# Output projection of a two-layer diffusion step: norms half a block apart, heads rounded straight out of PSUM, first inner block of the FFN in three token pieces

## The chip, the cores and the metric

The kernel runs on one core of a Trainium2 chip. The metric is the device time of one execution in microseconds (us), taken as the median of three runs. Five engines work side by side and meet at semaphores: PE (matrix multiplication, with its weight loads shown apart as PEld), DVE (vector), ACT (scalar functions and copies), POOL (a second, slower vector engine) and SP, whose queue issues the DMA transfers.

## The reference

One step of a two-layer model over 1152 tokens: 1024 latent tokens and a prompt of 128, width 1024. Layer 0 (in the names below l = 0) has differential attention, layer 1 sliding-window attention. What the change touches is what follows attention in each layer:

```python
o = rmsnorm(o, subln_g) * (1.0 - lam_init)         # layer 0 alone, one norm per head of 128
y = o @ w_o                                        # output projection, 1024 x 1024
x = x + gate1 * rmsnorm(y, g1)                     # post_norm_residual
h = rmsnorm(x, g2) * (1 + scale) + shift           # pre_norm_modulate
y = (silu(h @ w_gate) * (h @ w_up)) @ w_down       # SwiGLU, inner width 2816
x = x + gate2 * rmsnorm(y, g3)
```

## The kernel before

Tokens are worked on in nine blocks of 128, in the order `OORDER` = 0, 1, 4, 5, 2, 6, 3, 7, 8 (8 is the prompt). A program fixes the order on PE, ACT, DVE and POOL: what is written first in the code is issued first on its engine. Only the DMA queue is ordered by a scheduler.

Every fp32 operand of a large product is split in a rounded part ("h" in its name) and the rest ("l"), and a product is three matmuls: h by h, h by l, l by h.

**Output projection.** `OProj.step(i)` runs once for each of the nine places i, from -2 on, and lists its parts with an offset k, so that a step works on several blocks at once. `turn` of block i+1: eight PE transposes of the attention result V into the PSUM tile tp_o (L1312; tag "t", two banks), an ACT copy into the SBUF tile o32 (L1314 in layer 0, L1316 in layer 1), a rounding by POOL into oh (L110) and a DVE subtraction into ol (L1318). `norms(0)` of block i-1: sum of squares of the projected block by ACT (L127). `stat` of block i+2, in layer 0 alone: eight ACT squares, one per head (L1265). `proj` of block i: 48 matmuls in two halves (L1326 to L1328) into the PSUM tiles oacc. Between the halves `scale` (layer 0: square root, then POOL multiplies V by the head norms, L1281) and the norms of block i-1: `norms(1)` is a root (L135), a reciprocal (L137), DVE's scaling of oacc by two instructions (L153), POOL's or DVE's addition to the residual (L154) and the sum of squares of the result K by ACT (L127); `norms(2)` ends it on DVE (L145, L146) and gives xn. "Hooks" are pieces of other work hung on the halves of a step: the prompt's attention, the first pairs of tokens for the FFN (in steps 5 and 6), and the preparation of FFN weights.

**FFN, up.** 22 inner blocks d of 128 gate and 128 up columns. Instead of eight quarter products, each is worked out by seven (a Strassen form): names B11, B21, T2, T3, T1, B22, T4, into the PSUM tiles guX (tag "b", four banks), guY ("t", two) and guZ ("u", two). The tokens, folded in half, form two parts of 256 and 320 columns (`PARTS`). Weights are prepared by `prep`: for the Strassen sums POOL adds quarters (L1470 to L1477), ACT rounds (L1488) and DVE subtracts (fl, L1490), and the small "u" (L1480, L1481). For the tokens, `Halves.pair` takes two blocks: PE transposes xn into tp_n (L1388, two tiles, tag "u"), `first` rounds them by ACT (L1395) and copies them raw by DVE (L1396), `second` makes the sums and all rounded parts and rests (L1406 to L1421).

Part 0 (blocks 0, 4, 1, 5) is made in steps 5 and 6. Part 1 (blocks 2 with 6, 3 with 7, and the prompt) is made by the list `late` between the products of d = 0, part 0. Then d = 0 runs part 1, and from d = 1 on both parts follow each other product by product. `sums` takes the products out of PSUM (ACT L1534 to L1550, DVE L1536 to L1554).

Of the kernel before, what the change touches and what calls it, by code (L numbers as in the profile page):

```python
# [44 lines left out]
def hybrid_step(ctx: ExitStack, tc: tile.TileContext, x_prompt, x_sample, cache_diff_k, cache_diff_v,  # L45
# [1193 lines left out]
    class OProj:  # L1239
# [63 lines left out]
        def turn(self, tb):  # L1303
            i = OORDER.index(tb) % 2 * 2
            oh, ol = self.ohl[tb] = [self.room(f"w{i + f}", [P, KB, P], F32R, "oh") for f in range(2)]
            o32 = self.room("r1", [P, KB, P], F32, "o32")
            for half in range(2):
                ks = slice(half * 4, half * 4 + 4)
                tp = self.ps.tile([P, 4, P], F32, name="tp_o", tag="t", bufs=2)
                for j in range(4):  # L1310
                    kb = half * 4 + j
                    pe.transpose(tp[:, j, :], self.o[tb][:, kb * P:(kb + 1) * P], ident)  # L1312
                if self.l == 0:
                    act.activation(out=o32[:, ks, :], in_=tp, func=AF.Copy, scale=subg)  # L1314
                else:
                    act.copy(out=o32[:, ks, :], in_=tp)  # L1316
                pool_round(oh[:, ks, :], o32[:, ks, :])
                dve.tensor_tensor(out=ol[:, ks, :], in0=o32[:, ks, :], in1=oh[:, ks, :].bitcast(F32), op=ALU.subtract)  # L1318

# [10 lines left out]
        def norms(self, tb, part):  # L1330
            gg, G, sh = self.mod(tb)
            if part == 0:
                self.xn[tb] = self.room(f"x{OORDER.index(tb) % 5}", [P, D], F32, "xn")
                self.ss[tb] = sumsq(self.acc[tb], junk)
            elif part == 1:
                rs, x = rstd(self.ss[tb]), self.xt[tb]
                post_norm(self.acc[tb], rs, gg, x, x, self.xn[tb], dve if OORDER.index(tb) < 2 else pool)
                dma(out=x_d[tb * P:(tb + 1) * P, :], in_=x)
                self.ss[tb] = sumsq([x], junk)
            else:  # L1340
                pre_norm(rstd(self.ss[tb]), self.xt[tb], G, sh, self.xn[tb], dve)
# [21 lines left out]
    PARTS = (256, 320)  # L1363

    A_COLS = {(0, 0): ((0, 256, 0),), (0, 1): ((0, 256, 256),), (1, 0): ((0, 320, 512),),
              (1, 1): ((0, 256, 896), (256, 320, 832))}

    class Halves:
# [23 lines left out]
        def first(self, part, c, a, raw):  # L1392

            for i, name in enumerate(("B11", "B21")):
                act.copy(out=self.hi[name, part][:, :, c:c + a[i].shape[-1]], in_=a[i])  # L1395
                dve.tensor_copy(out=raw[:, i], in_=a[i])  # L1396

        def second(self, part, c, b, raws):
# [23 lines left out]
            high("T4", T)  # L1422
            for name, x in (("B11", B11), ("B21", B21), ("T1", T1), ("T2", T2), ("B22", B22), ("T4", T)):
                low(name, x)
# [18 lines left out]
    class Ffn:  # L1443
# [18 lines left out]
        def prep(self, d, what):  # L1462
# [15 lines left out]
            elif what == "u":  # L1478
                u = w[d, "u"] = rooms.take((P, D), F32R, "fhl")
                act.copy(out=u[:, 0:512], in_=A22)  # L1480
                dve.tensor_tensor(out=u[:, 512:D], in0=A22, in1=u[:, 0:512].bitcast(F32), op=ALU.subtract)  # L1481
                rooms.give(w[d, "r", 1])
# [16 lines left out]
        def product(self, d, k, part):  # L1499
            to, i, half, name = self.PRODUCTS[k]  # L1500
            n = PARTS[part]
            acc = self.acc

# [7 lines left out]
            if i == 1:  # L1511
                hi, lo = [self.w[d, "u"][:, f * 512:(f + 1) * 512] for f in range(2)]
# [3 lines left out]
            xh, xl = self.hv.hi[name, part], self.hv.lo[name, part]  # L1516
            for kb in range(4):
# [6 lines left out]
        def post(self, name, part):  # L1524
            t = self.pt.tile([P, 320], F32, name=name, tag=name, bufs={"s1": 3, "sg": 3 - self.l}.get(name, 2))
            return t[:, 0:PARTS[part]]

        def sums(self, d, k, part):

            acc, t, n = self.acc, self.sums_of.setdefault(part, {}), PARTS[part]  # L1530
            X, Y, Z = [acc[to, part][:, 0:n] if (to, part) in acc else None for to in "XYZ"]
# [30 lines left out]
        def free(self, d, k):  # L1562
            if k in self.DONE:
                self.rooms.give(*[self.w[d, f, self.DONE[k]] for f in "hl"])
            elif k == 6:
                self.rooms.give(self.w[d, "u"])

# [3 lines left out]
        def up(self, tasks, mroom, late, pt, ahead):  # L1571
# [161 lines left out]
    class Layer:  # L1733
# [8 lines left out]
        def begin(self, stack):  # L1742
# [15 lines left out]
            def pair(part, c, *tbs):  # L1758
                rooms = [where[f"x{OORDER.index(tb) % 5}"] for tb in tbs]
                yield from f.hv.pair(part, c, [op.xn[tb] for tb in tbs], [*rooms, *self.temps][:3])  # L1760
                if part:
                    f.rooms.free += rooms
                yield
# [11 lines left out]
            with tc.manual_schedule(engines=ENGINES):  # L1775
# [18 lines left out]
                f.rooms.free.insert(0, self.temps[0])  # L1794
# [9 lines left out]
        def ffn(self, tasks):  # L1804

            l, f, op, H = self.l, self.f, self.op, self.H
            with ExitStack() as high:
# [3 lines left out]
                for tag in names:  # L1811
# [4 lines left out]
                R.tile([P, 512], F32, name="room", tag="mw", bufs=2)  # L1816
                self.temps = [macc, (R, "mw", 2)]
# [183 lines left out]
```

## Time and profile before

| | |
|---|---|
| median of three runs | 3203.99 us (3201.15 to 3204.88) |
| the profiled execution's own time | 3199.07 us |
| its span in the trace | 3197.3 us |
| mean granted PE clock | 0.981 |
| PE busy | 3001.8 us, 94% of the span |
| DVE, ACT, POOL busy | 64%, 44%, 43% |
| longest chain | PE 67%, POOL 14%, DVE 9%, ACT 4% |

Times inside an execution are read in the trace as microseconds from the start of the span. The output projection of layer 0 with the first inner block behind it lies from about 834 to 1022.6 us, that of layer 1 from about 2264 to 2442.2 us. In 40 slices of the span the digit of PE falls to 8 in and behind these two places (and in the attention of layer 0).

### The profile page before, as it was taken

To read this page: it belongs to the slowest core of one execution; us is meant where nothing else is said; L and a number is where in the kernel's file an instruction comes from. 1 tells how busy PE (TensorE), PEld (TensorE's weight loads), DVE (VectorE), ACT (ScalarE), POOL (GpSimd) and SP (SyncE) were. 2 spreads that over 40 slices of the span, in tenths; PEclk is the share of its full clock that TensorE was granted. 3 is DMA by queue.
4 is the path that set the end of the run, shared out by engine and by line. 5 is a ranking of instruction groups with operands and counts; after the bars stand their busy time and mean duration, and the time that the engine had idled before them with its cause. 6 is when DMAs were issued, how large, how long until landed. Compare 5 with 4: busy or idle time off the path is not lost.

```text
span 3197.3 us, 47914 instructions
## 1 busy us (share of the span) xinstructions
PE 3001.8 (94%) x17998; PEld 2636.8 (82%) x17998; DVE 2048.6 (64%) x2789; ACT 1421.9 (44%) x2764; POOL 1361.9 (43%) x1186
## 2 busy tenths in 40 slices
PE   8999988998896999999999899999987999999999
PEld 5888777777776999999878787777767999998887
DVE  6786388888566777753786643999567633334544
ACT  6332267777554333333444323777433333333442
POOL 2553289999343444442021343666333433340101
PEclk9999999999998999999999999999988999999999
DMA  6675633332422434335765354433432322226564
GB/s 214 200 228 179 201 112 114 116 118 94 130 100 80 129 109 129 109 97 177 252 216 195 130 173 125 116 115 99 142 107 81 108 64 83 66 80 211 185 199 149
DMA packets 373808, 442.23 MB, mean 138 GB/s; under 512 B 26804, under 2 KB 295644, under 8 KB 373576
## 3 DMA queue, kind: packets, MB, share of 16 engines
q1 hardware_dynamic: 373576, 439.16, 43.6%
q8 instruction: 142, 2.33, 0.3%
q14 instruction: 90, 0.74, 0.1%
HBM read 335.71 MB, written 103.37 MB: 137 GB/s over the span
## 4 chain that ended last, share of the span: by engine, by line
PE 67%; POOL 14%; DVE 9%; ACT 4%; issue 3%; DMA 2%; SPq 1%; DVEq 0%; ACTq 0%; POOLq 0%
POOL aT L784 7%; PE guX L1518 6%; PE guX L1519 6%; PE guX L1520 6%; PE dacc L1635 5%; PE dacc L1637 5%; PE dacc L1636 5%; POOL aT L110 4%; PE qacc L556 4%; PE qacc L558 4%; PE qacc L557 4%; PE guY L1518 3%; PE guY L1520 3%; PE guY L1519 3%; PE guZ L1518 1%
## 5 line engine op out<-in xcount | busy, mean ns | idle before, releaser
L1551 POOL TENSOR_TENSOR sg<-sg,U 128x256 f32<-128x256 f32 x88 | 74.9, 851 | 563.4 <-ACT sg L1550 553.1
L1635 PE MATMUL dacc<-fh,ahl 128*128 128x512 f32 x792 | 312.0, 394 | 2.3 <-DVE U L1554 2.3
L1636 PE MATMUL dacc<-fl,ahl 128*128 128x512 f32 x792 | 310.7, 392 | 0.0
L1637 PE MATMUL dacc<-fh,ahl 128*128 128x512 f32 x792 | 310.7, 392 | 0.0
L556 PE MATMUL qacc<-whi,hh 128*128 128x512 f32 x648 | 259.7, 401 | 1.3 <-ACT hh L431 1.3
L558 PE MATMUL qacc<-whi,hl 128*128 128x512 f32 x648 | 254.9, 393 | 0.0
L557 PE MATMUL qacc<-wlo,hh 128*128 128x512 f32 x648 | 254.2, 392 | 0.6 <-DVE wlo L106 0.6
L154 POOL TENSOR_TENSOR xt<-yacc,xt 128x1024 f32<-128x1024 f32 (+1 forms) x19 | 49.7, 2621 | 459.9 <-DVE yacc L153 242.0
L784 POOL TENSOR_TENSOR aT<-a,aT 128x512 fp32r<-128x512 f32 x186 | 237.3, 1276 | 15.5
L1620 DVE TENSOR_TENSOR fl<-fraw,fh 128x1024 fp32r<-128x1024 f32 x132 | 165.4, 1253 | 121.3 <-ACT fh L1619 120.7
L744 DVE TENSOR_REDUCE nm<-S 128x1 f32<-128x1280 f32 x128 | 190.2, 1486 | 51.1 <-PE S L737 51.1
L1619 ACT CAST fh<-fraw 128x1024 fp32r<-128x1024 f32 x132 | 138.4, 1048 | 170.8 <-DMA fraw<-in_w_down_dram 156.7
L737 PE MATMUL S<-K,q 128*128 128x512 f32 (+1 forms) x768 | 184.5, 377 | 12.9 <-ACT e L749 8.9
L266 DVE SCALAR_TENSOR_TENSOR macc<-wmod,sc,macc 128x512 f32<-128x512 f32 x196 | 186.1, 992 | 0.0
L1635 PEld LDWEIGHTS dacc<-fh,ahl 128*128 128x128 f32 x792 | 149.2, 188 | 36.4 <-DVE U L1554 3.1
L1637 PEld LDWEIGHTS dacc<-fh,ahl 128*128 128x128 f32 x792 | 149.0, 188 | 33.7
L1636 PEld LDWEIGHTS dacc<-fl,ahl 128*128 128x128 f32 x792 | 149.1, 188 | 32.9
L749 ACT ACTIVATE e<-S,nm 128x1280 f32<-128x1280 f32 x128 | 171.4, 1339 | 7.2 <-DVE nm L744 7.1
L737 PEld LDWEIGHTS S<-K,q 128*128 128x128 f32 x768 | 137.5, 193 | 43.8 <-ACT e L749 19.0
L578 ACT CAST xT<-tpx 128x512 fp32r<-128x512 f32 x127 | 68.5, 592 | 236.5 <-issue 125.3
L110 POOL TENSOR_SCALAR aT<-a 128x512 fp32r<-128x512 f32 x192 | 154.0, 802 | 22.7 <-ACT a L773 22.7
L1490 DVE TENSOR_TENSOR fl<-fsum,fh 128x1024 fp32r<-128x1024 f32 x84 | 102.3, 1218 | 81.3 <-ACT fh L1488 81.3
(369 smaller groups left out, 9726.7 us busy)
## 6 DMA issues: line engine op xcount, KB each, us to landing
fraw<-in_w_down_dram SPq DMA_DIRECT2D x132, 512.0 KB
wmod<-in_w_mod_dram SPq DMA_DIRECT2D x112, 256.0 KB
araw<-a_d SPq DMA_DIRECT2D x132, 192.0 KB
fraw<-in_w_gate_dram SPq DMA_DIRECT2D x44, 512.0 KB
fraw<-in_w_up_dram SPq DMA_DIRECT2D x42, 512.0 KB
qT_d<-xT SPq DMA_DIRECT2D x36, 512.0 KB
q<-qT_d SPq DMA_DIRECT2D x64, 256.0 KB
wraw<-in_w_qkv_diff_dram SPq DMA_DIRECT2D x24, 512.0 KB
```

What stands on the lines that cost most here:

```text
L110: pool.tensor_scalar(out=out, in0=in_, scalar1=1.0, scalar2=0.0, op0=ALU.mult, op1=ALU.add)
L556: pe.matmul(acc, lhsT=xh, rhs=hi[:, a, :], start=(kb == 0), stop=False)
L557: pe.matmul(acc, lhsT=xh, rhs=lo[:, a, :], start=False, stop=False)
L558: pe.matmul(acc, lhsT=xl, rhs=hi[:, a, :], start=False, stop=(kb == KB - 1))
L737: pe.matmul(S[:, j:j + n], lhsT=self.q[:, f, m, i * P:(i + 1) * P], rhs=kv[self.h][0][:, m, j:j + n], start=(f == 0), stop=(f == 1))
L784: (dve if self.last else pool).tensor_tensor(out=lo, in0=x, in1=hi.bitcast(F32), op=ALU.subtract)
L1518: pe.matmul(o, lhsT=hi[:, kb, :], rhs=xh[:, kb, :], start=(first and kb == 0), stop=False, **more)
L1519: pe.matmul(o, lhsT=hi[:, kb, :], rhs=xl[:, kb, :], start=False, stop=False, **more)
L1520: pe.matmul(o, lhsT=lo[:, kb, :], rhs=xh[:, kb, :], start=False, stop=(kb == 3), **more)
L1635: pe.matmul(acc, lhsT=ah, rhs=hi[:, cs], start=(d == 0), stop=False)
L1636: pe.matmul(acc, lhsT=ah, rhs=lo[:, cs], start=False, stop=False)
L1637: pe.matmul(acc, lhsT=al, rhs=hi[:, cs], start=False, stop=(d == NDF - 1))
```

## The change

1. `turn` no longer has the tile o32 or POOL's rounding. ACT copies tp_o straight into oh, and DVE subtracts oh from tp_o in PSUM (one instruction that also scales, in layer 0).
2. In `step`, `norms(1)` stands right behind `norms(0)`, ahead of `stat`; `scale` stands ahead of the hooks in both layers, and `norms(2)` behind them.
3. The residual addition is on POOL for the blocks at places 2 to 6 and on DVE for places 0, 1, 7 and 8 (before: DVE for 0 and 1, POOL for the rest).
4. In `first` the raw copies are ACT's; in `second` the rest of T2 comes ahead of that of T1.
5. The weight preparation of d = 0 (`prep`) is regrouped: hg and lg in the first half of step 8, s1 in the second, ha and la ahead of the last block's norms, hb and lb behind `norms(1)`.
6. d = 0 runs in three views of the tokens: part 0 (256 columns), the first 256 columns of part 1, and its last 64 (the prompt's). All seven products are done for each, so that there are 84 more matmuls per layer, of 64 columns. The pairs of part 1 are spread over views 0 and 2 and the weights of d = 1 over views 2 and 3. Rooms and temporaries change to fit, and the intermediate a is stored by view.

```diff
@@ turn
-            o32 = self.room("r1", [P, KB, P], F32, "o32")
...
+                hi, lo = oh[:, ks, :], ol[:, ks, :]
                 if self.l == 0:
-                    act.activation(out=o32[:, ks, :], in_=tp, func=AF.Copy, scale=subg)
+                    act.activation(out=hi, in_=tp, func=AF.Copy, scale=subg)
+                    dve.scalar_tensor_tensor(out=lo, in0=tp, scalar=subg, in1=hi.bitcast(F32), op0=ALU.mult,
+                                             op1=ALU.subtract)
                 else:
-                    act.copy(out=o32[:, ks, :], in_=tp)
-                pool_round(oh[:, ks, :], o32[:, ks, :])
-                dve.tensor_tensor(out=ol[:, ks, :], in0=o32[:, ks, :], in1=oh[:, ks, :].bitcast(F32), op=ALU.subtract)
+                    act.copy(out=hi, in_=tp)
+                    dve.tensor_tensor(out=lo, in0=tp, in1=hi.bitcast(F32), op=ALU.subtract)
@@ norms
-                post_norm(self.acc[tb], rs, gg, x, x, self.xn[tb], dve if OORDER.index(tb) < 2 else pool)
+                post_norm(self.acc[tb], rs, gg, x, x, self.xn[tb], pool if 2 <= OORDER.index(tb) < 7 else dve)
@@ step
-                    (0, "load_x"), (1, "turn"), (3 - self.l, "load"), (-1, "norms", 0), (2, "stat", 0), (2, "stat", 1),
-                    (0, "proj", 0), *(((None, 0), (2, "scale")), ((None, 0), (2, "scale")))[self.l],
-                    (-1, "norms", 1), (-1, "norms", 2), (0, "proj", 1), (None, 1)):
+                    (0, "load_x"), (1, "turn"), (3 - self.l, "load"), (-1, "norms", 0), (-1, "norms", 1), (2, "stat", 0),
+                    (2, "stat", 1), (0, "proj", 0), (2, "scale"), (None, 0), (-1, "norms", 2), (0, "proj", 1),
+                    (None, 1)):
@@ Halves.first
-                dve.tensor_copy(out=raw[:, i], in_=a[i])
+                act.copy(out=raw[:, i], in_=a[i])
@@ Ffn.up, d == 0
-                    for i, k in enumerate((0, 1, 2, 4, 3, 5, 6)):
-                        self.product(0, k, 0)
-                        for f in late[i] if i < len(late) else ():
-                            f()
-                    for k in range(7):
-                        self.product(0, k, 1)
-                        self.free(0, k)
-                        self.ahead(1, k)
+                    for view in (0, 2, 3):
+                        for i, k in enumerate((0, 1, 2, 4, 3, 5, 6)):
+                            self.product(0, k, view)
+                            if view == 3:
+                                self.free(0, k)
+                            for f in late.get((view, i), ()):
+                                f()
@@ the layer: preparation of d = 0
-                hooks[8, 0] = [lambda: prep("s0", "hg")]
-                hooks[8, 1] = [lambda: prep("s1", "lg")]
+                hooks[8, 0] = [lambda: prep("s0", "hg", "lg")]
+                hooks[8, 1] = [lambda: prep("s1")]
...
+                prep("ha", "la")
                 op.norms(TB_PROMPT, 0)
-                prep("hb", "ha", "la")
                 op.norms(TB_PROMPT, 1)
-                prep("lb")
+                prep("hb", "lb")
                 op.norms(TB_PROMPT, 2)
...
                 prep("u")
@@ the layer: late
-                late = [[], [lambda: step(pairs[0])], [lambda: step(pairs[0], 2), lambda: f.fetch(1)],
-                        [lambda: step(pairs[1])], [lambda: step(pairs[1], 2)], [], [lambda: step(pairs[2], 2)]]
+                late = {(0, 0): [pair(0)], (0, 2): [pair(0, 2)], (0, 4): [pair(1)],
+                        (0, 6): [pair(1, 2), lambda: f.fetch(1)], (2, 1): [pair(2, 2)],
+                        (2, 3): prep("s0"), (2, 4): prep("s1"), (2, 6): prep("hg"),
+                        (3, 1): prep("lg", "ha"), (3, 3): prep("la", "hb"), (3, 5): prep("lb"),
+                        (3, 6): prep("u") + [lambda: f.fetch(2)]}
```

Two places show the new order. The first is ACT in a middle step of layer 0's output projection; L1314 is the copy of tp_o, L127 with oacc is `norms(0)`, L127 with K belongs to `norms(1)`, L1265 is `stat`. Before:

```order
L931 COPY pf<-tpa 128x512
L1314 ACTIVATE o_9008<-tp_o,subg 128x512 x2
L127 ACTIVATE junk,ss<-oacc 128x512 x2
L1265 ACTIVATE junk,ss_9032<-V 128x128 x8
L943 COPY pf<-av 128x512
L1277 ACTIVATE ss_9032<-ss_9032,eps_t 128x8
L135 ACTIVATE ss<-ss,eps_t 128x1
L127 ACTIVATE junk,ss<-K 128x1024
```

The same step of the changed kernel:

```order
L931 COPY pf<-tpa 128x512
L1314 ACTIVATE oh<-tp_o,subg 128x512 x2
L127 ACTIVATE junk,ss<-oacc 128x512 x2
L135 ACTIVATE ss<-ss,eps_t 128x1
L127 ACTIVATE junk,ss<-K 128x1024
L1265 ACTIVATE junk,ss_9023<-V 128x128 x8
L1277 ACTIVATE ss_9023<-ss_9023,eps_t 128x8
L943 COPY pf<-av 128x512
L135 ACTIVATE ss<-ss,eps_t 128x1
```

The root and the sum over K moved from behind the eight squares to ahead of them.

The second is ACT where the last block's norms meet the first product of the FFN in layer 0; L1534 (L1542 in the changed kernel) is the first product leaving PSUM, the casts to fhl and B11h are "u" and `first`. Before:

```order
L1534 COPY s_9711<-guX 128x256
L127 ACTIVATE junk,ss<-K 128x1024
L135 ACTIVATE ss<-ss,eps_t 128x1
L1480 CAST fhl<-V 128x512
L1395 CAST B11h<-tp_n 128x4x128
L1395 CAST B21h<-tp_n 128x4x128
L1539 COPY U_9754<-guX 128x256
```

The same place of the changed kernel:

```order
L1542 COPY s_9684<-guX 128x256
L135 ACTIVATE ss<-ss,eps_t 128x1
L127 ACTIVATE junk,ss<-K 128x1024
L1495 CAST fh<-K 128x1024
L135 ACTIVATE ss<-ss,eps_t 128x1
L1487 CAST fhl<-V 128x512
L1399 CAST B11h<-tp_n 128x4x128
L1400 COPY raw<-tp_n 128x512
L1399 CAST B21h<-tp_n 128x4x128
L1400 COPY raw<-tp_n 128x512
L1547 COPY U_9727<-guX 128x256
```

One weight cast and the two raw copies joined this stretch of ACT; the casts and copies still stand behind the last block's norms. On PE the transposes tp_n of the first pair of part 1 moved from behind the second product (guZ) to ahead of it.

## Rows read from the trace of the kernel before

**Rows 1.** Windows: stretch, length, busy us of PE, PEld, DVE, ACT, POOL, granted clock.

```profile
967.51:1022.58 55.07, 33.68 (x207) 32.11 (x207) 39.05 (x58) 24.17 (x46) 12.11 (x9) 0.82 0.20 63
2386.30:2442.17 55.87, 36.21 (x207) 34.68 (x207) 39.05 (x58) 24.10 (x46) 12.09 (x9) 0.78 0.21 65
```

**Rows 2.** What PE waited for, layer 0, 790 to 1060 us: total, times, longest.

```profile
PE tp_n L1388 <- DVE raw L1396: 10.1, 3, 5.4
PE guX L1519 <- DVE B11l L1409: 9.4, 1, 9.4
PE guX L1520 <- DVE fl L1490: 7.4, 1, 7.4
PE tp_o L1312 <- POOL V L1281: 6.4, 2, 4.7
PE tp_n L1388 <- DVE s L1536: 2.7, 1, 2.7
```

**Rows 3.** Timeline of ACT, POOL and DVE in one step of layer 0.

```profile
886.75 1.28 ACT L1314 ACTIVATE o<-tp_o,subg 128x512 f32<-128x512 f32 x2
889.04 0.34 ACT L1265 ACTIVATE junk<-V 128x128 f32<-128x128 f32 x1
892.42 0.56 ACT L943 COPY pf<-av 128x512 f32<-128x512 f32 x1
898.38 1.06 ACT L127 ACTIVATE junk<-K 128x1024 f32<-128x1024 f32 x1 [4.67 <-POOL K L154]
...
894.10 1.90 POOL L1281 TENSOR_TENSOR V<-V,rs 128x1024 f32<-128x1024 f32 x1 [2.76 <-ACT ss L135]
895.95 2.39 POOL L154 TENSOR_TENSOR K<-xn,K 128x1024 f32<-128x1024 f32 x1
...
894.07 1.41 DVE L153 SCALAR_TENSOR_TENSOR xn<-oacc,rs,q 128x512 f32<-128x512 f32 x2
```

**Rows 4.** Timeline of PE, layer 0: turns of three blocks and the last projection.

```profile
899.13 1.04 PE L1312 MATMUL tp_o<-ident,V 128*128 128x128 f32 x8
899.93 0.48 PE L1326 MATMUL oacc<-woh,oh 128*128 128x512 f32 x1
...
912.93 1.04 PE L1312 MATMUL tp_o<-ident,V 128*128 128x128 f32 x8
...
931.37 1.97 PE L1312 MATMUL tp_o<-ident,V 128*128 128x128 f32 x8 [1.72 <-POOL V L1281]
...
948.46 0.47 PE L1326 MATMUL oacc<-woh,oh 128*128 128x512 f32 x1 [2.46 <-DVE xn L153]
```

**Rows 5.** Timeline of PE: neighbours of 256 columns (layer 0) and of 320 (layer 1).

```profile
1030.03 0.28 PE L1518 MATMUL guX<-T2h,fh 128*128 128x256 f32 x1
1030.15 0.28 PE L1519 MATMUL guX<-T2l,fh 128*128 128x256 f32 x1
...
2441.73 0.31 PE L1518 MATMUL guY<-T4h,fhl 128*128 128x320 f32 x1
2441.88 0.31 PE L1519 MATMUL guY<-T4l,fhl 128*128 128x320 f32 x1
```

**Rows 6.** Timeline of DVE and ACT, layer 0, at the start of d = 0.

```profile
970.65 1.22 DVE L1490 TENSOR_TENSOR fl<-V,fh 128x1024 fp32r<-128x1024 f32 x1 [2.04 <-ACT fh L1488]
978.55 1.28 DVE L145 SCALAR_TENSOR_TENSOR xn<-K,rs,bc 128x1024 f32<-128x1024 f32 x1
984.36 0.69 DVE L1412 TENSOR_TENSOR raw<-tp_n,raw 128x512 f32<-128x512 f32 x1 [1.47 <-PE tp_n L1388]
987.68 0.68 DVE L1409 TENSOR_TENSOR B11l<-raw,B11h 128x512 fp32r<-128x512 f32 x1
...
979.87 0.62 ACT L1480 CAST fhl<-V 128x512 fp32r<-128x512 f32 x1 [1.60 <-DVE xn L145]
980.39 0.58 ACT L1395 CAST B11h<-tp_n 128x512 fp32r<-128x512 f32 x1
980.87 0.59 ACT L1395 CAST B21h<-tp_n 128x512 fp32r<-128x512 f32 x1
```

**Rows 7.** Timeline of PE, layer 1: the last projection and a matmul behind it.

```profile
2367.29 0.76 PE L1326 MATMUL oacc<-woh,oh 128*128 128x512 f32 x1 [5.97 <-DVE xn L153]
2386.31 0.58 PE L1520 MATMUL guX<-B11h,fl 128*128 128x256 f32 x1 [4.55 <-DVE fl L1490]
```

More of the change, by code (lines that the diff above doesn't have):

```diff
@@ L1363, in hybrid_step @@
     PARTS = (256, 320)
+    VIEWS = ((0, 0, 256), (1, 0, 320), (1, 0, 256), (1, 256, 320))
     A_COLS = {(0, 0): ((0, 256, 0),), (0, 1): ((0, 256, 256),), (1, 0): ((0, 320, 512),),
-              (1, 1): ((0, 256, 896), (256, 320, 832))}
+              (1, 1): ((0, 256, 896), (256, 320, 832)), (2, 0): ((0, 256, 512),), (2, 1): ((0, 256, 896),),
+              (3, 0): ((0, 64, 768),), (3, 1): ((0, 64, 832),)}
     class Halves:
@@ L1422, in second @@
             high("T4", T)
-            for name, x in (("B11", B11), ("B21", B21), ("T1", T1), ("T2", T2), ("B22", B22), ("T4", T)):
+            for name, x in (("B11", B11), ("B21", B21), ("T2", T2), ("T1", T1), ("B22", B22), ("T4", T)):
                 low(name, x)
@@ L1478, in prep @@
             elif what == "u":
-                u = w[d, "u"] = rooms.take((P, D), F32R, "fhl")
-                act.copy(out=u[:, 0:512], in_=A22)
-                dve.tensor_tensor(out=u[:, 512:D], in0=A22, in1=u[:, 0:512].bitcast(F32), op=ALU.subtract)
+                if (d, "u") not in w:
+                    u = w[d, "ur"] = rooms.take((P, D), F32R, "fhl")
+                    w[d, "u"] = u[:, 0:512], u[:, 512:D]
+                hi, lo = w[d, "u"]
+                act.copy(out=hi, in_=A22)
+                dve.tensor_tensor(out=lo, in0=A22, in1=hi.bitcast(F32), op=ALU.subtract)
                 rooms.give(w[d, "r", 1])
@@ L1500, in product @@
             to, i, half, name = self.PRODUCTS[k]
-            n = PARTS[part]
-            acc = self.acc
+            src, c0, c1 = VIEWS[part]
+            n, acc = c1 - c0, self.acc
             first = k in (0, 1, 3)
@@ L1511, in product @@
             if i == 1:
-                hi, lo = [self.w[d, "u"][:, f * 512:(f + 1) * 512] for f in range(2)]
+                hi, lo = self.w[d, "u"]
             else:
@@ L1515, in product @@
             hi, lo = [x.rearrange("p (a n) -> p a n", n=P) for x in (hi, lo)]
-            xh, xl = self.hv.hi[name, part], self.hv.lo[name, part]
+            xh, xl = [x[name, src][:, :, c0:c1] for x in (self.hv.hi, self.hv.lo)]
             for kb in range(4):
@@ L1525, in post @@
             t = self.pt.tile([P, 320], F32, name=name, tag=name, bufs={"s1": 3, "sg": 3 - self.l}.get(name, 2))
-            return t[:, 0:PARTS[part]]
+            return t[:, 0:VIEWS[part][2] - VIEWS[part][1]]
         def sums(self, d, k, part):
-            acc, t, n = self.acc, self.sums_of.setdefault(part, {}), PARTS[part]
+            acc, t = self.acc, self.sums_of.setdefault(part, {})
+            n = VIEWS[part][2] - VIEWS[part][1]
             X, Y, Z = [acc[to, part][:, 0:n] if (to, part) in acc else None for to in "XYZ"]
@@ L1565, in free @@
             elif k == 6:
-                self.rooms.give(self.w[d, "u"])
+                if (d, "ur") in self.w:
+                    self.rooms.give(self.w[d, "ur"])
         def begin(self, rooms):
@@ L1759, in pair @@
                 rooms = [where[f"x{OORDER.index(tb) % 5}"] for tb in tbs]
-                yield from f.hv.pair(part, c, [op.xn[tb] for tb in tbs], [*rooms, *self.temps][:3])
+                temps = self.temps + [where["x4"]]
+                yield from f.hv.pair(part, c, [op.xn[tb] for tb in tbs], [*rooms, *temps][:3])
                 if part:
-                    f.rooms.free += rooms
+                    f.rooms.free += [r for r in rooms if r != where["x4"] or len(tbs) == 1]
+                    if len(tbs) == 1:
+                        f.rooms.free.append(where["x4"])
                 yield
@@ L1789, in begin @@
                 hooks[7, 0] = [first]
-                hooks[8, 0] = [lambda: prep("s0", "hg")]
-                hooks[8, 1] = [lambda: prep("s1", "lg")]
+                hooks[8, 0] = [lambda: prep("s0", "hg", "lg")]
+                hooks[8, 1] = [lambda: prep("s1")]
                 for i in range(-2, NTB):
                     op.step(i, hooks)
-                f.rooms.free.insert(0, self.temps[0])
+                f.rooms.free = [where["w0"], where["w1"], where["r1"], self.temps[0]]
+                prep("ha", "la")
                 op.norms(TB_PROMPT, 0)
-                prep("hb", "ha", "la")
                 op.norms(TB_PROMPT, 1)
-                prep("lb")
+                prep("hb", "lb")
                 op.norms(TB_PROMPT, 2)
@@ L1816, in ffn, with pair, prep @@
                 R.tile([P, 512], F32, name="room", tag="mw", bufs=2)
-                self.temps = [macc, (R, "mw", 2)]
+                self.temps = [macc]
                 pt = high.enter_context(sbuf(f"pt{l}", "right"))
                 pairs = [self.pair(1, c, *tbs) for c, tbs in ((0, (2, 6)), (P, (3, 7)), (2 * P, (TB_PROMPT,)))]
-                late = [[], [lambda: step(pairs[0])], [lambda: step(pairs[0], 2), lambda: f.fetch(1)],
-                        [lambda: step(pairs[1])], [lambda: step(pairs[1], 2)], [], [lambda: step(pairs[2], 2)]]
+                def pair(i, n=1):
+                    return lambda: step(pairs[i], n)
+                def prep(*whats):
+                    return [lambda what=what: f.prep(1, what) for what in whats]
+                late = {(0, 0): [pair(0)], (0, 2): [pair(0, 2)], (0, 4): [pair(1)],
[3 more added lines that the diff above has]
+                        (3, 6): prep("u") + [lambda: f.fetch(2)]}
                 def switch():
```

## The prediction

> **What bounds the kernel now.** I read the table of busy times first: PE is busy for 94% of the span, so a change can win only where PE stands idle or runs slowly. The waits of PE, grouped by what ended them, put that idle time in one place per layer, the end of the output projection and the first inner block d = 0. In layer 0 PE waits there 9.4 us for the rest of B11 of part 1, 10.1 us in three pieces for DVE's raw copies, 7.4 us for the first weight rest, 2.7 us for DVE's first sum, and 6.4 us in two pieces earlier on for POOL's scaling of V [rows 2]. In layer 1 the last projection waits 5.97 us for DVE's scaling of oacc and the first product 4.55 us for its weight rest [rows 7]. The windows by stretch show the rest: from the third matmul of d = 0 to the first of d = 1, layer 0 takes 55.07 us for 33.68 us of PE work, at a mean granted clock of 0.82, and layer 1 55.87 us for 36.21 at 0.78 [rows 1]. So some 21 and 20 us are waits, and part of the work runs at the 1.2 GHz level. That is the most the change could reach there. DVE with 39.05 us of 55 is the busiest of the helpers in both stretches.
>
> **Heads out of PSUM.** POOL's rounding and the tile o32 go, and PE gets oh some microseconds earlier: a turn now is transposes, ACT copy, DVE subtraction. No wait of PE in [rows 2] names a turn's oh, so this pays only through POOL's free time. DVE now reads PSUM; the raw sum that reads tp_n takes 0.69 for 512 columns and the rest that reads SBUF 0.68 [rows 6], so I put the difference at nothing. The bank of tp_o is free only after DVE's read; DVE has idle time before it in the step, and I put that at nothing too, with 1 us per step as the upper bound if a bank comes late.
>
> **The two norms half a block apart, layer 0.** This is the part I cost above nothing. In one step of before, the ACT chain is: two copies from 886.75, then the sums over oacc, the eight squares of `stat` from 889.04 to 892.42 (3.38 us), 1.68 us of small steps to POOL's scaling at 894.10, and 1.90 us of scaling; V is ready at 896.0 and PE turns it at 899.13 [rows 3, 4]. That is a slack of 3.1 us. The change puts `norms(1)` ahead of the squares on ACT: a root and a reciprocal (0.7), DVE's scaling 1.41, the addition 2.39 on POOL, the sum over K 1.06 and its root [rows 3], together 5.8 us, during which ACT, in order, can do nothing of `stat`. For this step V is 5.8 later against a slack of 3.1, so PE waits 2.7 us, and since each step's turn starts the next chain, the delay does not shrink: the chain of a step is 0.7 + 2.3 + 5.8 + 3.4 + 1.7 + 1.9 = 15.8 us, where PE's own step takes 13.8 (899.13 to 912.93 [rows 4]). The last turn, at 931.37, already waited 1.72 for V [rows 4] and so takes the whole 5.8. My sums put the six turns at -2.6, +1.4, +6.8, +5.9, +8.0 and +13.3 us against before. The first gains, because POOL has no rounding to do ahead of the scaling. Behind the last turn two waits vanish: the 2.46 us of the last projection [rows 4], whose DVE scaling now comes early, and most of the 7.4 us for the weight rest [rows 2], as lg is now ahead of `norms(2)`. What is left is **+4.2 us** at the third matmul of d = 0 (967.5 to 971.7). Bounds: 0 if ACT's waits fall where the hooks waited anyway, so that the removed 9 us pay in full and the chain costs only as much; +13 if the 7.4 us stay.
>
> **The same, layer 1.** There is no `stat`, so nothing stands behind the new sum on ACT but the prompt's exponentials and the copies; I put two delays of some 3 us there, at most half of which lies on PE's path. The wait of 5.97 us goes, as `norms(1)` now stands at the head of the step, and the 4.55 us go with lg [rows 7]. 10.5 less 3 to 6 gives **-6 us** (bounds -9 and 0).
>
> **d = 0 in three views.** 84 matmuls of 64 columns are added, and 84 get 256 instead of 320 columns. At full clock a matmul of 320 columns follows the one before by 0.147 us, one of 256 by 0.12 [rows 5], and eight transposes of 128 take 0.80, 0.10 each [rows 4]. From 256 to 128 the price falls only by 0.02, so I take 0.10 for 64: 8.4 us added, 2.3 saved, +6.1 per layer. Bounds per matmul: 0.05, half of the row for 128, and 0.12; so +1.9 to +7.8.
>
> The waits: the raw copies leave DVE (six per layer of 0.6 us) for ACT. The transposes of the first pair are now ahead of guZ, and all three tiles share the tag of two banks, so guZ must wait until `first` has read them. ACT does `first` only behind the last block's norms and the cast to fhl, as before (979.87, after DVE's L145 [rows 6]). With the last projection's end 4.2 later I lay it out: B11 done 972.9, root, scaling 1.41, addition by DVE 1.22 (as a DVE row of that size), sum 1.06, a weight cast 1.0, root, L145 1.28, cast 0.62, four copies at 0.5: guZ starts near 983.5, after a wait of about 10 us that takes the place of 8 us before the second tp_n and of the following ones. From there: six products at 12 x 0.12, three sets of transposes at 0.8 and some 2 us of bank waits end part 0 at 996.5. View 2 waits about 3.5 us for B11's rest (4.0 from the first DVE sum of a pair to that row's end [rows 6]) in place of 9.4; seven products and a set of transposes end it at 1011, and view 3, whose tokens are ready by then, at 1019.5. With 3 us for stretches at the low clock d = 0 takes 51 us. If each of the later products also waits for its rest or for a bank (T1 2.5, T4 and U4 some 2 each, and the half clock longer), it takes 59. Both ends rest on rows of another order, so I take 54 for both layers: **-1 us** in layer 0, **-2** in layer 1, with 48 and 59 as bounds.
>
> **The sum** is +4.2 - 6 - 1 - 2 = -5, and with 1 us of bank waits per layer put back **-3 us**. The profiled execution took 3199.07 by its own time, 4.9 below the median of 3203.99; applied to the median that is 3201.
>
> A page of the Trainium skill prices small matmuls otherwise. "TensorE: Matmul & The Clock Gate", section "Back-to-back issue gap", gives the isolated gap as columns divided by 2.4 per ns, plus 2.5 ns, 29 ns for 64 columns, though it says itself that at few columns this leaves out the weight load. By that the view would add 2.4 us instead of 8.4; the rows for 128 columns (0.10, against 56 ns by the formula) speak against it.
>
> **Rivals.**
> A. Waits traded for small matmuls and for the chain in layer 0, as above: 3201, own range 3194 to 3210.
> B. The waits go. guZ isn't late, because ACT reaches `first` as early as PE does, and the chain of layer 0 only fills time in which PE waited anyway. Then d = 0 takes 47 us in both layers (40 of PE work, 7 of waits), -17, and layer 1's -6 stands, layer 0's entry at 0: 3204 - 23 = 3181; half of that, 3192, where one of the two holds. For it: DVE is freed of the raw copies that PE waits for by name. Against: ACT, in program order, has the last block's norms ahead of `first`.
> C. Slower by the chain in front of `stat`. If the weight rest still ends late, and each step of layer 0 loses its full 5.8 less 3.1 with the low clock behind each wait, the entry of layer 0 is at +13 and d = 0 at 59 in both: 13 - 6 + 4 + 3 = +14: 3218. It decides once the chain exceeds PE's step, 13.8 us, by over 2 us; my sum says 2.0.
> D. Small matmuls cost their columns (0.03 to 0.05 each): 84 x 0.05 to 0.07 x 2 = 8 to 12 less: 3191.
>
> **How the numbers follow.** A 0.45, B 0.25, C 0.22, D 0.08. A measurement of this kernel can tell a change of about 0.2%, 6.4 us, from none. A gives mostly no change (0.33 of its 0.45; 0.09 faster, 0.03 slower); B is faster but for 0.02, D faster but for 0.02; C is slower but for 0.03. Faster 0.38, same 0.40, slower 0.22. The range that leaves out no more than 2 in 10 runs from half of B's way, 3184, to C's 3218.
>
> **What would show it.** Right: in layer 0 PE waits at the turns for POOL's V in most steps and the squares follow the sum over K; the last projection and the third matmul of d = 0 wait for nothing long in either layer; PE's largest wait in d = 0 is guZ for ACT's copies, near 10 us; small matmuls follow each other by 0.10. Wrong: turns of layer 0 at their old spacing, guZ without a wait, or view 3 below 5 us (then the gain is larger); or a wait for the weight rest that stays, with low clock on both sides (then it is slower).

## The result and the profile after

The changed kernel takes 3231.31 us (median of 6 runs, 3228.81 to 3233.67) against 3201.61 for the kernel before: a ratio of 1.009, 95% interval 1.0077 to 1.0103. It is slower by 30 us, outside the predicted range. The profiled execution has a span of 3227.7 us, 30.4 more than before.

The windows from the third matmul of d = 0 to the first of d = 1, which answer to [rows 1], show where most of it went (the columns are stretch, length, busy us of PE, PEld, DVE, ACT and POOL, granted clock; layer 0 first):

```profile
972.03:1040.57 68.54, 43.43 (x290) 41.98 (x291) 40.44 (x58) 27.32 (x60) 14.28 (x11) 0.79 0.21 67
2402.74:2471.29 68.55, 47.02 (x290) 45.40 (x291) 40.57 (x58) 27.07 (x60) 13.84 (x11) 0.73 0.22 70
```

The stretch grew from 55.07 to 68.54 us in layer 0 and from 55.87 to 68.55 in layer 1: 13.5 and 12.7 us. PE's busy time grew by 9.7 and 10.8 us, so only a few of these are additional waits.

What PE waited for in layer 0, 790 to 1060 us, answers to [rows 2]:

```profile
PE guZ L1525 <- ACT raw L1400: 13.3, 1, 13.3
PE tp_n L1392 <- ACT raw L1400: 8.9, 3, 8.3
PE tpa L929 <- DVE rs L137: 6.6, 1, 6.6
PE guX L1526 <- DVE B11l L1413: 4.0, 1, 4.0
PE tp_o L1311 <- POOL V L1281: 3.1, 3, 1.3
PE guX L1525 <- ACT U L1547: 2.7, 2, 2.4
```

The 7.4 us for the weight rest, the 9.4 for B11's rest and the 10.1 for DVE's raw copies of [rows 2] are gone or small. In their place stand 13.3 us in one wait of guZ for ACT's raw copies, 8.3 us at the transposes of a token pair right ahead of the last turn, and 6.6 us at the prompt's transposes (868.94). The profile puts this last one down to a reciprocal of the norms; the exponential that these transposes need comes on ACT at 865.70, and it now stands behind the norms and the squares.

Timeline rows of PE at the places of [rows 4], and at the third matmul of d = 0:

```profile
889.05 0.33 PE L1311 MATMUL tp_o<-ident,V 128*128 128x128 f32 x1 [1.00 <-POOL V L1281]
905.43 0.47 PE L1311 MATMUL tp_o<-ident,V 128*128 128x128 f32 x1 [1.34 <-POOL V L1281]
...
921.99 0.33 PE L1311 MATMUL tp_o<-ident,V 128*128 128x128 f32 x1
...
945.37 0.63 PE L1311 MATMUL tp_o<-ident,V 128*128 128x128 f32 x2
...
972.03 0.39 PE L1527 MATMUL guX<-B11h,fl 128*128 128x256 f32 x1 [0.76 <-DVE fl L1497]
```

The turns that began at 899.13, 912.93 and 931.37 in the kernel before now begin at 905.43, 921.99 and 945.37: later by 6.3, 9.1 and 14.0 us. At the third matmul of d = 0 only 4.5 of that is left. In layer 1 the first turn of the stretch is 19.8 us later than in the kernel before and the third matmul 16.4, so the projection there gained 3.4 us.

The windows of d = 0 in layer 0 by stage: up to guZ, up to the end of view 2's wait for the rest of B11, the rest of view 2, view 3 in two pieces, and the start of d = 1:

```profile
972.03:987.70 15.67, 2.33 (x18) 2.09 (x18) 12.89 (x14) 5.58 (x14) 4.45 (x2) 0.66 0.28 101
987.70:1008.36 20.66, 13.48 (x98) 12.84 (x98) 12.28 (x22) 12.23 (x23) 1.46 (x2) 0.91 0.29 90
1008.36:1025.17 16.81, 12.52 (x91) 12.08 (x92) 11.01 (x18) 5.84 (x16) 7.32 (x5) 0.91 0.00 1
1025.17:1028.34 3.17, 3.17 (x32) 3.17 (x30) 0.72 (x3) 0.75 (x3) 0.73 (x1) 1.00 0.26 83
1028.34:1040.57 12.23, 11.93 (x57) 11.79 (x57) 3.55 (x4) 2.93 (x7) 0.32 (x1) 0.50 0.25 73
1040.57:1045.41 4.84, 4.84 (x21) 4.84 (x22) 2.71 (x4) 0.37 (x1) 4.14 (x4) 0.50 0.33 94
```

View 3, the 84 matmuls of 64 columns, begins at 1025.17 at the full 2.4 GHz. In the midst of these matmuls, without a gap ahead, the granted clock falls to 0.50 (1.2 GHz), though PE goes on with all but no wait, and it stays there for the rest of the view and for the first 4.84 us of d = 1. Two rows of PE on either side of the fall show the price of one:

```profile
1027.10 0.28 PE L1525 MATMUL guZ<-B21h,fh 128*128 128x64 f32 x1
1027.21 0.28 PE L1526 MATMUL guZ<-B21l,fh 128*128 128x64 f32 x1
...
1030.55 0.40 PE L1526 MATMUL guX<-T1l,fh 128*128 128x64 f32 x1
1030.76 0.40 PE L1527 MATMUL guX<-T1h,fl 128*128 128x64 f32 x1
```

One follows the other by 0.11 us at the full clock and by 0.21 behind the fall. Layer 1 shows the same: the clock is 1.00 for the first 2.88 us of the view and 0.50 from 2458.52 on, for the other 12.77 us of the view and the first 4.30 of d = 1.

### The profile page after: what moved, and what is told of

The parts are those of the page before. It is cut to its first block, busy times and chain, and to the rows that moved or that the text cites. A ratio compares the mean times of both kernels' runs of the same rounds, so it can differ in the third digit from the quotient of the medians.

```text
span 3227.7 us, 48289 instructions
## 1 busy us (share of the span) xinstructions
PE 3023.9 (94%) x18166; PEld 2658.4 (82%) x18166; DVE 2040.5 (63%) x2779; ACT 1437.8 (45%) x2796; POOL 1326.0 (41%) x1150
## 5 line engine op out<-in xcount | busy, mean ns | idle before, releaser
L1559 POOL TENSOR_TENSOR sg<-sg,U 128x256 f32<-128x256 f32 (+2 forms) x90 | 75.2, 836 | 591.4 <-ACT sg L1558 535.3
L737 PEld LDWEIGHTS S<-K,q 128*128 128x128 f32 x768 | 135.6, 190 | 43.0 <-ACT e L749 18.8
```

The lines of the kernel that those rows point to most:

```text
L737: pe.matmul(S[:, j:j + n], lhsT=self.q[:, f, m, i * P:(i + 1) * P], rhs=kv[self.h][0][:, m, j:j + n], start=(f == 0), stop=(f == 1))
```

## The experiments

The theory after the result: the third piece is the larger part of the loss, through the low clock that the 64-column matmuls bring and through their number. The rivals: guZ's wait behind the moved transposes; ACT's longer queue (raw copies); the norm order, whose loss of 4.5 us at the third matmul may hide a larger one, since the regrouped weights gain there at the same time.

All times below are compared with the kernel before, run beside it on the same chip (medians 3200.78 to 3201.89). The changed kernel was not run again beside them, so differences against it are differences of medians; by the intervals of the ratios such a difference is good to some 5 to 7 us, and the traces say where it lies.

**Two views (e1).**

```diff
-                    for view in (0, 2, 3):
+                    for view in (0, 1):
...
-                        (0, 6): [pair(1, 2), lambda: f.fetch(1)], (2, 1): [pair(2, 2)],
...
+                        (0, 6): [pair(1, 2), lambda: f.fetch(1), pair(2, 2)]}
```

> The changed kernel with d = 0 in two views again (256 and 320 columns), the pairs of part 1 all made in the first, the weights of d = 1 behind the second; all else as changed. If the third piece is what costs (84 small matmuls per layer and the low clock from 1028 us on), d = 0 falls from 68.5 to about 56 us in each layer and the time by 20 to 25 us, to about 3208. If the wait of guZ and the new order on ACT cost, it stays within 6 us of 3231, since both are kept here.

Measured: 3212.15 us, ratio 1.0033 (1.0023 to 1.0042), 19 us faster than the changed kernel. The windows of d = 0, layer 0 and layer 1:

```profile
973.24:1033.74 60.50, 32.72 (x206) 30.84 (x207) 40.46 (x56) 26.35 (x55) 13.31 (x9) 0.77 0.21 68
2396.42:2455.59 59.17, 33.89 (x207) 31.89 (x208) 40.42 (x56) 26.23 (x55) 12.86 (x9) 0.77 0.24 73
```

d = 0 is 8.0 and 9.4 us shorter than in the changed kernel, and d = 1 begins at the full clock. So the third piece, with the places of pairs and weights that come with it, costs more than it takes away; yet 60 us is longer than the 55 of [rows 1], so it is not the only loss in d = 0.

**The same number of matmuls, twice as wide (e2).**

```diff
-    VIEWS = ((0, 0, 256), (1, 0, 320), (1, 0, 256), (1, 256, 320))
+    VIEWS = ((0, 0, 256), (1, 0, 320), (1, 0, 256), (1, 192, 320))
...
```

`A_COLS` changes with it, so that only the last 64 of the 128 columns are stored.

> The changed kernel, but its third view works on 128 columns (64 of them a second time), so as many matmuls of twice the width. If it is the 64 columns that make the granted clock fall to half from 1028 us on, the clock stays at 1.0 there, the view takes about 9 us instead of 15.4 and d = 1 starts at full clock: 7 to 9 us less per layer, about 3215. If the clock falls because of the waits in the view before, it falls here too and the time is the same or 1 us more.

Measured: 3217.75 us, ratio 1.0054 (1.0039 to 1.0069): 13.6 us faster than the changed kernel, with twice the columns in that view. The windows of view 3 and of the start of d = 1, layer 0 and layer 1, and two rows of PE in the view:

```profile
1029.38:1039.28 9.90, 9.54 (x86) 9.40 (x85) 4.41 (x6) 3.91 (x9) 1.19 (x3) 1.00 0.27 82
1039.28:1045.87 6.59, 6.59 (x52) 6.59 (x52) 2.32 (x5) 1.75 (x3) 4.42 (x4) 1.00 0.46 129
2452.85:2462.75 9.90, 9.54 (x86) 9.40 (x85) 4.41 (x6) 3.81 (x9) 1.19 (x3) 1.00 0.41 118
2462.75:2469.30 6.55, 6.55 (x51) 6.55 (x51) 3.36 (x5) 1.75 (x3) 5.90 (x5) 1.00 0.30 76
...
1030.67 0.27 PE L1525 MATMUL guZ<-B21h,fh 128*128 128x128 f32 x1
1030.78 0.27 PE L1526 MATMUL guZ<-B21l,fh 128*128 128x128 f32 x1
```

The clock stays at 1.00 through the view and behind it. The waits in the view before are all but the same (in layer 0 2.4 us for ACT as there, 1.6 for DVE against 1.9), so these don't make it fall. Nor is it a chance of two layers: e3, e4 and e8 below keep the 64 columns, and in both layers of each, as in the changed kernel, the clock falls to 0.50 between 2.9 and 6.2 us behind the start of that view. A matmul of 128 columns here follows the one before by 0.11 us, just as one of 64 did at the full clock: the view costs by the number of its matmuls, and 64 columns save nothing while bringing the low clock. Of the 19 us that e1 won about 13 are the clock (by the traces 5.1 and 6.5 in d = 0 and some 4 behind it). The other 6 are what e1 and e2 differ by: the 84 additional matmuls per layer, but also the places of pairs and weights, which no run separates.

**The first pair behind guZ (e3).**

```diff
-                late = {(0, 0): [pair(0)], (0, 2): [pair(0, 2)], (0, 4): [pair(1)],
+                late = {(0, 1): [pair(0)], (0, 2): [pair(0, 2)], (0, 4): [pair(1)],
```

> The changed kernel with the transposes of the first pair behind guZ instead of ahead of it, as they stood before the change. If guZ's wait for the two banks (13.3 and 9.8 us) costs, it goes, and d = 0 gets 5 to 10 us shorter per layer: 3213 to 3221. If ACT's place behind the last block's norms sets the end, the same wait stands at the next transposes instead, and the time moves by less than 4 us.

Measured: 3224.21 us, ratio 1.0076 (1.0059 to 1.0093): 7 us faster than the changed kernel. guZ follows the first product without a wait, and two shorter waits stand at the transposes, as PE's rows show:

```profile
972.13 0.28 PE L1525 MATMUL guZ<-B21h,fh 128*128 128x256 f32 x1
...
977.68 0.48 PE L1392 MATMUL tp_n<-ident,xn 128*128 128x128 f32 x1 [3.51 <-DVE s L1544]
...
986.72 0.47 PE L1392 MATMUL tp_n<-ident,xn 128*128 128x128 f32 x1 [5.35 <-ACT raw L1400]
```

Of the 13.3 us of guZ's wait 8.9 come back here; d = 0 is 64.1 us against 68.5. Both theories were half right: the place costs 4.5 to 5 us per layer, the rest is ACT's late `first`.

**The old order in a step (e4).**

```diff
-                    (0, "load_x"), (1, "turn"), (3 - self.l, "load"), (-1, "norms", 0), (-1, "norms", 1), (2, "stat", 0),
-                    (2, "stat", 1), (0, "proj", 0), (2, "scale"), (None, 0), (-1, "norms", 2), (0, "proj", 1),
-                    (None, 1)):
+                    (0, "load_x"), (1, "turn"), (3 - self.l, "load"), (-1, "norms", 0), (2, "stat", 0), (2, "stat", 1),
+                    (0, "proj", 0), *(((None, 0), (2, "scale")), ((None, 0), (2, "scale")))[self.l],
+                    (-1, "norms", 1), (-1, "norms", 2), (0, "proj", 1), (None, 1)):
```

> The changed kernel with the order of parts in a projection step as before (the norms together behind the hooks, stat ahead of them). If the norm chain in front of stat costs layer 0 what the two traces show (4.5 us at the third matmul of d = 0) and layer 1 gains some 2, the time falls by about 3 us plus the low clock, 3225 to 3229. If the order is what pays for the rest, the last projections wait again (6 us in layer 1) and the time rises to 3235 or more.

Measured: 3213.32 us, ratio 1.0039 (1.0024 to 1.0054): 18 us faster than the changed kernel, against some 2 to 6 expected. From the first turn to the third matmul of d = 0 it takes 142.6 us in layer 0, where the changed kernel takes 155.4 and the kernel before 150.2, and 129.9 us in layer 1 (136.8 and 140.2). So the norm order costs 12.8 and 6.9 us, and other edits in the same stretch gain 7.6 and 10.3; the comparison of the two traces alone showed only the difference. The first turn and the third matmul of layer 0 in PE's rows here:

```profile
818.70 0.49 PE L1311 MATMUL tp_o<-ident,V 128*128 128x128 f32 x3
...
961.33 0.28 PE L1527 MATMUL guX<-B11h,fl 128*128 128x256 f32 x1
```

These sums hold to some 2 us: e1, e2 and e3, which keep the changed order, take 155.3 to 155.9 and 135.5 to 136.0 there, and e5, e6 and e10 below, with the old order, 142.4 to 144.8 and 129.5 to 130.5. The last projection of layer 1 does wait again, 4.59 us, and costs less than the order that avoids it.

**The other edits alone (e5).** The changed kernel with the old order, two views and the pair behind guZ:

```diff
-                    for view in (0, 2, 3):
+                    for view in (0, 1):
...
-                late = {(0, 0): [pair(0)], (0, 2): [pair(0, 2)], (0, 4): [pair(1)],
-                        (0, 6): [pair(1, 2), lambda: f.fetch(1)], (2, 1): [pair(2, 2)],
...
+                late = {(0, 1): [pair(0)], (0, 2): [pair(0, 2)], (0, 4): [pair(1)],
+                        (0, 6): [pair(1, 2), lambda: f.fetch(1), pair(2, 2)]}
...
-                    (0, "load_x"), (1, "turn"), (3 - self.l, "load"), (-1, "norms", 0), (-1, "norms", 1), (2, "stat", 0),
...
+                    (0, "load_x"), (1, "turn"), (3 - self.l, "load"), (-1, "norms", 0), (2, "stat", 0), (2, "stat", 1),
...
```

(the tuple of `step` as in e4)

> Of the change only the heads out of PSUM, the residual addition by DVE at places 7 and 8, the raw copies by ACT and the regrouped preparation of d = 0; the order in a step, the place of the first pair (behind guZ) and the two views are as before. If the order in a step, the third piece and the place of the pair are what cost, the entry of e4 stays (third matmul of d = 0 some 10 us earlier against the first turn than in the kernel before, in both layers) and d = 0 takes about 55 us: 3185 to 3192, faster than before. If the raw copies by ACT hold d = 0, it takes 60 us or more and the time is near that of before.

Measured: 3186.53 us, ratio 0.995 (0.9936 to 0.9963): 15 us faster than before. The three parts taken back gave 18, 19 and 7 us each alone by the medians, 44 together; all three give 44.8 (by the ratios, 12.2 thousandths against 14.0, each ratio with an interval of 1 to 1.7 to either side). They add up within what can be measured; each was also undone alone, so each is a cause by itself. Against the first turn, the third matmul comes 5.5 us earlier than before in layer 0 and 10.6 in layer 1. d = 0 takes 59.6 and 55.1 us. PE's waits in layer 0:

```profile
PE tp_n L1392 <- ACT raw L1400: 11.3, 2, 8.3
PE guX L1526 <- DVE B11l L1413: 7.8, 1, 7.8
PE tp_o L1311 <- POOL V L1281: 7.2, 3, 4.7
PE guX L1527 <- DVE fl L1497: 3.8, 1, 3.8
```

**Raw copies by DVE again (e6)**, in that kernel:

```diff
-                act.copy(out=raw[:, i], in_=a[i])
+                dve.tensor_copy(out=raw[:, i], in_=a[i])
```

> The kernel of e5_mix with the raw copies on DVE as before. If ACT's longer queue at the first pair (four copies instead of two) costs, this is 2 to 6 us faster than e5_mix; if DVE is the one that PE waits for there, as in the waits of before, it is 4 to 10 us slower.

Measured: 3186.68 us, 0.9951 (0.9938 to 0.9963): the same. In layer 0 PE's longest wait at the transposes changes its name, from 8.3 us for ACT's raw copies to 8.1 for DVE's, and not its length; in layer 1 it grows from 3.8 to 8.1 us. d = 0 takes 56.3 and 56.2 us against 59.6 and 55.1. Neither expectation held: over the whole, the engine that copies makes no difference that can be measured. That the work which both engines have ahead of the copies is what is late would explain it, but no run shows that by itself.

**The new order alone (e7)**, in the kernel before.

```diff
-                    (0, "load_x"), (1, "turn"), (3 - self.l, "load"), (-1, "norms", 0), (2, "stat", 0), (2, "stat", 1),
...
+                    (0, "load_x"), (1, "turn"), (3 - self.l, "load"), (-1, "norms", 0), (-1, "norms", 1), (2, "stat", 0),
...
```

(and the rest of the tuple as in the change)

> The kernel before with one edit, the new order of parts in a projection step. If the norm chain in front of stat costs, the turns of layer 0 move as in the changed kernel (+6 to +9 in the middle steps, +13 at the last) and the time rises by 8 to 20 us. If the cost seen in e4 lies in its meeting with the other edits, the time stays within 6 us of before.

Measured: 3220.01 us, 1.0055 (1.0041 to 1.0069): 18 us slower than before, the same size as e4 found from the other side. The last turn of layer 0 comes 18.8 us later against the first turn, the third matmul 14.3; in layer 1 the third matmul 4.8.

**The old turn (e8)**, in the changed kernel: the tile o32, POOL's rounding and the subtraction from o32 are put back.

```diff
-                    act.activation(out=hi, in_=tp, func=AF.Copy, scale=subg)
-                    dve.scalar_tensor_tensor(out=lo, in0=tp, scalar=subg, in1=hi.bitcast(F32), op0=ALU.mult,
-                                             op1=ALU.subtract)
+                    act.activation(out=o32[:, ks, :], in_=tp, func=AF.Copy, scale=subg)
...
+                pool_round(oh[:, ks, :], o32[:, ks, :])
+                dve.tensor_tensor(out=ol[:, ks, :], in0=o32[:, ks, :], in1=oh[:, ks, :].bitcast(F32), op=ALU.subtract)
```

> The changed kernel with the turn as before (o32, rounding by POOL). I put the edit at nothing: no wait of PE named it. If so, the time stays within 5 us of the changed kernel; if the freed POOL pays in the chain to V of layer 0 (its rounding stands ahead of the scaling), the turns there come 2 to 3 us later each and the time rises by 6 us or more.

Measured: 3240.2 us, 1.0117 (1.0103 to 1.0131): 9 us slower than the changed kernel, so the new turn is a gain. DVE's timeline in one step shows the way:

```profile
896.03 1.52 DVE L146 TENSOR_TENSOR xn<-xn,bc 128x1024 f32<-128x1024 f32 x1
899.32 1.69 DVE L1318 TENSOR_TENSOR oh<-o,oh 128x512 fp32r<-128x512 f32 x2 [1.78 <-POOL oh L110]
900.94 0.14 DVE L130 TENSOR_TENSOR ss<-ss 128x1 f32<-128x1 f32 x1
901.44 0.17 DVE L137 RECIPROCAL rs<-ss 128x1 f32<-128x1 f32 x1 [0.36 <-ACT ss L135]
901.65 1.41 DVE L153 SCALAR_TENSOR_TENSOR xn<-oacc,rs,q 128x512 f32<-128x512 f32 x2
```

The rest of the heads waits 1.78 us for POOL's rounding, and the norm's reciprocal and scaling stand behind it on DVE. With the norms at the head of the step this wait is in the chain to the next turn.

**Early norms in the last two steps alone (e9)**, added to e5: the changed tuple for i of 7 and 8, the old one for i below 7.

> The kernel of e5_mix with the changed order of parts in the last two steps alone (places 7 and 8), where no stat of layer 0 is left to stand behind the norms. If the early norms cost only through stat and the hooks of the middle steps, the last projections no longer wait for DVE's scaling (2.6 and 4.6 us in e5_mix) and the time falls by 3 to 7 us to 3180 to 3184. If ACT is what the last steps lack, the wait moves to the transposes of step 7 or to the turn, and the time is that of e5_mix.

Measured: 3187.3 us, 0.9957 (0.9944 to 0.9971): no different from e5. The last projection of layer 0 waits 1.5 us for DVE's scaling instead of 2.6, but the first DVE sum (5.0 us) and a weight cast (2.1) are waited for behind it; in layer 1 the wait of 4.6 us stays. There DVE does all sums and rests of a token pair (2348.97 to 2355.88) ahead of the scaling that PE waits for, at 2357.79; the order of the norms in the step doesn't touch that queue.

**POOL's addition at places 7 and 8 (e10)**, in e5 (`dve if OORDER.index(tb) < 2 else pool`, as before).

> The kernel of e5_mix with the residual addition by POOL at places 7 and 8 as before. If it is the faster addition (1.2 us by DVE against 2.4 by POOL) at the end of the projection that brings part of the gain, the first transposes of part 1 come 2 us later per layer and the time rises by 3 to 5 us; if the regrouped weights alone bring it, it stays within 2 us of e5_mix.

Measured: 3188.74 us, 0.9965 (0.9952 to 0.9979). The median is 2 us above e5 and the intervals overlap: too little to tell.

**The new turn alone (e11)**, in the kernel before.

> The kernel before with one edit, the new turn (heads rounded by ACT straight out of PSUM, no work of POOL). From e8, where the old turn cost the changed kernel 9 us, this would be 5 to 9 us faster than before; if the turn only helps where the norm chain stands in front of stat, it is within 3 us of before.

Measured: 3196.4 us, 0.9985 (0.9976 to 0.9994): 4.5 us faster. Against the first turn, the third matmul of d = 0 comes 1.1 us earlier than before in layer 0 and 3.8 in layer 1. It is a small gain by itself; the 9 us of e8 look larger, but by the ratios the two gains are 1.5 and 2.7 thousandths with some 0.9 and 1.9 to either side, so it isn't shown that the turn gains more with the new norm order.

## Why the prediction was wrong

**The step that failed** is "so I take 54 for both layers: -1 us in layer 0, -2 in layer 1, with 48 and 59 as bounds". d = 0 took 68.5 us in both, so that these two terms, -3 together, measured +26.2 (13.5 and 12.7). Some 4 more lie behind it, where d = 1 starts at the low clock: 21 matmuls take 4.84 us and 19 take 4.30, where the 0.127 each of e2's start of d = 1 would make 2.7 and 2.4. By the stages of the lay-out in layer 0:

- Up to guZ I had 11.8 us, and it took 15.7. The mechanism was right, guZ waits for ACT's `first` behind the last block's norms, and "near 10 us" was 13.3. What I left out stands on DVE: the end of the previous block's norms (L145 and L146, from 972.09 to 974.63) and the rest of the second weight (2.28 us at 974.55) are ahead of the sum that the norm's root waits for (L130, 976.75), and ACT's timeline shows that root at 978.00, where I had it right behind the first product:

```profile
973.52 0.37 ACT L1542 COPY s<-guX 128x256 f32<-128x256 f32 x1 [0.51 <-PE guX L1527]
978.00 0.29 ACT L135 ACTIVATE ss<-ss,eps_t 128x1 f32<-128x1 f32 x1 [4.10 <-DVE ss L130]
981.29 1.06 ACT L127 ACTIVATE junk<-K 128x1024 f32<-128x1024 f32 x1 [3.00 <-DVE K L154]
986.06 0.62 ACT L1487 CAST fhl<-V 128x512 fp32r<-128x512 f32 x1 [2.49 <-DVE xn L145]
986.59 0.58 ACT L1399 CAST B11h<-tp_n 128x512 fp32r<-128x512 f32 x1
```

- From guZ to the rest of B11, 16.5 expected and 20.7 measured; view 2, 11 and 16.8. Here are the single bank waits that I had named for the upper bound (1.8, 1.3, 1.9 and 2.4 us) and a clock of 0.91.
- View 3, 8.5 expected and 15.4 measured. The price at the full clock was right, 0.11 against 0.10. I had not thought that matmuls in an unbroken row could bring the low clock, and had 3 us for it in the whole of d = 0. e2 shows that this alone is worth some 13 us over both layers.

**The chain in front of `stat`, layer 0: right in its steps, its size hidden.** The six turns were predicted at -2.6, +1.4, +6.8, +5.9, +8.0 and +13.3 us and came at -2.6, +2.1, +6.8, +6.3, +9.1 and +14.0; the third matmul at +4.2 and came at +4.5. ACT's timeline has the predicted order, with eight squares behind the sum over K (897.49, 898.67). POOL ends V at 889.00, 905.38, 921.93 and 945.07, right ahead of the last four turns, at 889.05, 905.43, 921.99 and 945.37. Yet PE's waits name V for 3.1 us alone, because two other waits fill the same time: the turn at 869.81 came behind the 6.6 us at the prompt's transposes, with V ready at 866.98, and the last one behind 8.3 us for ACT's raw copies, which stand behind the same squares. What I didn't draw from the sum is that the order itself costs the 12.8 us that e4 measured, and that the other edits of the stretch carry it: of their 7.6 us e11 shows 1.1 for the turn, and no run separates the regrouped weights from the additions.

**Layer 1's -6** came as -3.4. The wait of 5.97 us went and that for the weight rest fell to 0.8, but on ACT the sum over K (2289.84) now stands ahead of the prompt's exponential (2292.30). The prompt's transposes at L1207 wait 4.0 us for it, until 2292.99, and the granted clock is 0.50 from 2291.3 to 2298.1. The prediction had "two delays of some 3 us there, at most half of which lies on PE's path"; that allows 3 us at most, so -7.5, where the sum took off 3 to 6. What it left out as well: the root and the exponential alternate more often in the new order, and ACT loads a function table nine times in this projection instead of seven (1.28 us each, nine in every run that has the new order throughout, seven in all others). How much of that reaches PE is not shown. e4 shows the order as a loss of 6.9 us there too. The gain of 10.3 is that of the other edits, 3.8 of it the turn's (e11).

**Heads out of PSUM at nothing** was too low: e8 and e11 give a gain of 9 and 4.5 us. I had looked for a wait of PE that named oh and found none; it is DVE that waits for POOL's rounding, with the norms behind it.

**The raw copies at ACT** changed nothing measurable (e6), as the sum had it. **Rival C**, slower by the chain, was the nearest in sign, with another place: the loss it priced at d = 0 (+4 and +3) was 13 in each layer, and its +13 at the entry of layer 0 was 4.5. **Rival D**, that small matmuls cost their columns, is refuted by the 0.11 us of 64 and of 128 columns. The formula of the Trainium skill ("TensorE: Matmul & The Clock Gate", section "Back-to-back issue gap") for an isolated gap makes 29 ns for 64 columns, an estimate, and the section says itself that at few columns the formula counts too little because it leaves out the weight load. The trace agrees with that reservation: 0.11 us in this stream of matmuls, each with its own weight load.

What stays open: whether e5's third matmul in layer 0, 5.5 us earlier than before and not 7.6 as in e4, differs by more than chance (e6 and e10 have 7.8 and 6.9 there), and which of the additions and weights carries what part of the remaining gain (e10 was too small to tell).

## What to carry to other kernels

A change that moves a consumer earlier on an in-order engine is costed by what it pushes back on that engine: here eight squares behind a chain over DVE, POOL and ACT, once per step. Two edits in one stretch can hide each other; the loss of 12.8 us showed as 4.5 in the traces, and only undoing one of them showed it. Cutting a stage into pieces as narrow as these is priced by the number of matmuls, here 0.11 us each at the full clock and 0.21 at the low one, and here it brought the low clock as well, into the stretch behind too.

## What the hardware showed that was not expected

PE's granted clock fell from 1.00 to 0.50 in the middle of an unbroken row of 64-column matmuls, at 1028.34 us in layer 0 and at 2458.52 in layer 1; with 128 columns in the same places, as many matmuls and all but the same waits ahead of them (e2), it did not. In the three other runs with 64 columns (e3, e4, e8) it fell in both layers. A matmul of 64 columns and one of 128 follow the one before by the same 0.11 us at the full clock.
